# Five re-orderings on single engines in a one-core trunk layer: a gate pair's products, the rounding of k, two copies, one gated product

## The chip, the cores and the metric

The kernel runs on one core of one Trainium2 chip. The time is the device time of one execution in microseconds (us), and of several executions the median is taken. The core's engines run side by side: TensorE (PE in the profile) multiplies matrices, with its weight load shown apart as PEld; VectorE (DVE) and ScalarE (ACT) do elementwise work; GpSimd (POOL) does some elementwise work and issues some of the transfers; SyncE (SP) issues most of them. Each engine works through its own instruction list in order, and waits at an instruction until what it needs has been signalled.

## The reference, cut to what matters

One layer of a streaming encoder, on 512 tokens of 1024 channels, all in float32:

```
h    = rms_norm(x);   xa, ga, q, k, v, f, gA, gB = split(h @ w_in)
y_a  = gelu(ga) * rg_lru(causal_conv4(xa))              # recurrent branch, width 1280
y_b  = softmax(q k^T / 8 + cum[i] - cum[j], causal) @ v  # 16 heads of 64
m    = sigmoid(gA + bA) * (y_a @ w_proj_a) + sigmoid(gB + bB) * (y_b @ w_proj_b)
x    = x + rms_norm(m @ w_out)
u    = causal_conv3(rms_norm(x) @ w_up)                  # 1024 -> 6144
gate, val = split(u)
x    = x + rms_norm((gelu(gate) * val) @ w_down)         # 3072 -> 1024
```

The change touches four products: `h @ w_in` for the gates gA and gB, q and k of the attention, `@ w_up`, and the last block of `gelu(gate) * val`, which is an input of `@ w_down`.

## The kernel before, in words

**High and low halves.** Every float32 operand of a matmul is split in two tiles: a rounded one (`h`, cast on ACT) and the remainder (`l`, subtracted on DVE: value minus rounded value). A product takes three matmuls: high by high, high by low, low by high. Each block of weights therefore passes through an SP transfer into a `raw_` tile, an ACT cast into `wh_` and a DVE subtraction into `wl_` (class `Split`). `fetch(i)` issues these three for all blocks up to number i of one long list; `unit(name)` takes a block for use and fetches two blocks beyond it, so for q of pair p + 1 that of pair p + 2. In some stages the remainder comes in another way (`plain_low`): ACT writes the negated raw tile into `ml`, and a transfer on POOL's queue adds the raw data onto it.

**Products in pairs.** Gates and up-projection take two output tiles (128 channels by 512 tokens each) together as a `Pair`, with seven products of half the inner size in place of eight, from sums of weight blocks (`sums`, tiles `t`, `th`, `tl`) and sums of inputs (`sh`, `sl`). Each product is 12 matmuls of 256 columns (L405, L406, L408). They go into two PSUM banks, `p.a` and `p.c`. Between them intermediate results are copied out by ACT (`keep`, L412, tiles `x0`, `x1`, `x2`; `gx` in the gates) and added back by DVE (`add`, L424). `p5` starts bank `c`; `p12` does products 1 and 2 in bank `a`, of which `keep(2)` then copies one half, and `add` adds it to the other before `product(6)` goes on there. One `period` (L429) interleaves the products of pair p with the last product and the epilogue of the pair before (`b`), and with the splitting of the weights of the next two (`n1`, `n2`). In the first period there is no pair before it (`b` is empty). In the gates (L911 to L945) and in the up-projection (from L1315) the order of all instructions on each engine is the order in which the program issues them (a manual schedule).

**Attention.** It runs over eight pairs of heads, p = 0 to 7. In each turn `scores` (L980) multiplies q and k of pair p, q and k of pair p + 1 are projected (`project`, 24 matmuls of 512 columns each, L218 to L220), and then `halves` (L963) turns the finished PSUM banks into `h_q`, `l_q`, `h_k`, `l_k`: a rounding copy on ACT (L966) and a subtraction on DVE (L967). `scores` of the next pair needs all four. It multiplies high by high, high by low and low by high into three banks per head (`s0a`, `s0b`, `s0c` for head 0). Here the order on each engine isn't written by hand: the tile layer's planner sets it, from the program's order and what it reckons to be ready. `prep_alloc` prepares the attention's biases, `tg_load` loads gate tiles that `gate_epilogue` had stored as `gmb`.

**Up-projection and down-projection.** The epilogue of an up pair is a convolution of three taps (ACT L1267, DVE L1273), a GELU on ACT (L1277), and `glu` (L1279): the product of both halves on POOL (L1281, tile `yf`), stored to DRAM (`yd`) by a transfer on SP's queue, for the last block, j = 23, on POOL's. The down-projection is 42 steps of 12 matmuls (L1387 to L1389). Step i needs its weights (`wh_dn`, `wl_dn`) and its inputs `ah` and `al`, split by ACT (L1361) and DVE from tiles loaded back out of `yd` (`yr` for the first six steps, and `q` or its sums behind them).

Of the kernel before, what the change touches and what calls it, by code (L numbers as in the profile page):

```python
# [12 lines left out]
ALU = mybir.AluOpType  # L13
# [12 lines left out]
JF = DF // P  # L26
# [37 lines left out]
def kernel(  # L64
# [16 lines left out]
    act, dve, pool, pe = nc.scalar, nc.vector, nc.gpsimd, nc.tensor  # L81
# [3 lines left out]
    def offset(stack, n, side="left"):  # L85

        places[0] += 1
        pool = stack.enter_context(tc.tile_pool(name=f"offset{places[0]}", bufs=1, side=side))
        pool.tile([P, n // 4], F32, name=f"offset{places[0]}")
# [9 lines left out]
    def bank(name):  # L99
        return pspools[-1].tile([P, 512], F32, tag="ps", name=name)  # L100
# [98 lines left out]
    where = {name: i for i, (name, _, _) in enumerate(order)}  # L199
    ready, emitted, special = {}, [0], {}  # L200

    def fetch(i):
        while emitted[0] <= min(i, len(order) - 1):
            n, src, shape = order[emitted[0]]
            w = Split(src, shape, n, special.get(n))
            w.hi()
            w.lo(dve)
            ready[n] = w.parts()
            emitted[0] += 1

    def unit(name, ahead=2):

        i = where[name]
        fetch(i + ahead)
        return ready.pop(name)

    def mm3(dst, ah, al, bh, bl, first, last):
        pe.matmul(dst, ah, bh, start=first, stop=False)  # L218
        pe.matmul(dst, ah, bl, start=False, stop=False)  # L219
        pe.matmul(dst, al, bh, start=False, stop=last)  # L220

    def project(dst, unit, ah, al, lo=0, hi=S):
        wh, wl = unit
        for k in range(KD):
            mm3(dst[:, lo:hi], wh[:, k], wl[:, k], ah[:, k, lo:hi], al[:, k, lo:hi], k == 0, k == KD - 1)
# [56 lines left out]
    hh = hpool.tile([P, KD, S], F32R, name="hh")  # L282
    hl = hpool.tile([P, KD, S], F32R, name="hl")
# [32 lines left out]
    def sub(out, a, b):  # L316
        dve.tensor_tensor(out=out, in0=a, in1=b, op=ALU.subtract)  # L317

    A, B = slice(0, 512), slice(512, 1024)
    X, Y = slice(0, SH), slice(SH, S)  # L320
# [109 lines left out]
    def period(p, b, n1, n2, epilogue, load):  # L430

        if b:
            p.p5()
            b.add(b.c[:, Y], b.a[:, Y], 1)
            b.add(b.c[:, X], b.c[:, X], 0)
        n1.plain(1)
        if b:
            epilogue(b, "c", 0)
            p.keep(1, p.c[:, X])
            n1.sums(0)  # L440
        p.product(6, p.a[:, Y])
        if b:
            n1.sums_hi(0)
        p.keep(0, p.a[:, Y])
        if b:
            epilogue(b, "c", 1)
            n1.sums(1)
            b.product(4, b.a[:, Y])
            epilogue(b, "a", 0)
            n1.sums_lo(0)  # L450
        n2.plain_low(0)
        if b:
            n1.sums_hi(1)
        p.product(3, p.c[:, X])
        if b:
            epilogue(b, "a", 1)
        n2.plain_high(0)
        n1.p12()
        if b:
            n1.sums_lo(1)  # L460
        if isinstance(n1, Pair):
            n1.keep(2, n1.a[:, Y])
        if b:
            epilogue(b, "a", 2)
        if isinstance(n1, Pair):
            n1.add(n1.a[:, X], n1.a[:, X], 2)
        load()
        epilogue(b, "a", 3)
        p.product(7, p.a[:, Y])

    with ExitStack() as rg:
        rt, ixt, tt = {}, {}, {}
        last_act = [None]
        with ExitStack() as r0:
# [208 lines left out]
            for t in range(NF, TR + NF):  # L683
# [3 lines left out]
                if t < TR:  # L687
                    ps = bank(f"xa{t}")
# [154 lines left out]
        for step, (e, half) in enumerate(PA_ORDER):  # L843
# [3 lines left out]
            for i in range(5):  # L847
                k = 5 * half + i
# [48 lines left out]
    with ExitStack() as g2:  # L897
        spool = g2.enter_context(tc.tile_pool(name="gsums", bufs=1, side="right", reuse_waits="tile"))
        gates.sh = [spool.tile([P, KH, SH], F32R, name=f"gsh{i}") for i in range(4)]
        gates.sl = [spool.tile([P, KH, SH], F32R, name=f"gsl{i}") for i in range(4)]  # L900
        gp[1] = Pair(gates, 1, GP[1])
        man = g2.enter_context(ExitStack())
        man.enter_context(tc.manual_schedule())
        for i, f in enumerate((fq[3], fq[0], fq[2], fq[1])):
            act.copy(gates.sh[i], f)
            sub(gates.sl[i], f, gates.sh[i].bitcast(F32))
        hfstk.close()
        st0pool = splitstk.enter_context(tc.tile_pool(name="gsplit0", bufs=2, side="right", reuse_waits="tile"))
        offset(splitstk, 448, "right")
        st1pool = splitstk.enter_context(tc.tile_pool(name="gsplit1", bufs=2, side="right", reuse_waits="tile"))  # L910
        gates.stpools = [st0pool, st1pool]  # L911
        none = Nothing()
        p, n = gp[0], gp[1]
        p.plain_high(0)
        p.plain_high(1)
        p.p5()
        p.p12()
        n.sums(0)
        n.sums(1)
        n.plain_low(0)  # L920
        p.keep(2, p.a[:, Y])
        p.add(p.a[:, X], p.a[:, X], 2)
        p.keep(1, p.c[:, X])
        n.sums_hi(0)
        n.sums_lo(0)
        n.sums_hi(1)
        n.sums_lo(1)
        n.plain_high(0)
        gp[2] = Pair(gates, 2, GP[2])

        def more(j):
            if j + 3 < len(GP):
                gp[j + 3] = Pair(gates, j + 3, GP[j + 3])
            elif j + 2 < len(GP):
                pass
            else:
                fetch(where[("q0", "k0")[j + 2 - len(GP)]])

        for j in range(len(GP)):
            period(gp[j], gp.get(j - 1), gp.get(j + 1, none), gp.get(j + 2, none), gate_epilogue, lambda: more(j))  # L940
            gp.pop(j - 1, None)
        splitstk.close()
        sumstk.close()
        bpool = bstk.enter_context(tc.tile_pool(name="bias", bufs=2, reuse_waits="tile"))
        bias = prep_alloc(0)  # L945
        b = gp.pop(len(GP) - 1)
        b.add(b.c[:, Y], b.a[:, Y], 1)
        b.add(b.c[:, X], b.c[:, X], 0)
        gate_epilogue(b, "c", 0)
        pq = bank("q0")  # L950
        project(pq, unit("q0", 0), hh, hl)
        gate_epilogue(b, "c", 1)
        pk = bank("k0")
        project(pk, unit("k0", 0), hh, hl)
        b.product(4, b.a[:, Y])
        gate_epilogue(b, "a", 0)
        gate_epilogue(b, "a", 1)

    with ExitStack() as at:
# [3 lines left out]
        def halves(ps, name):  # L963
            hi = apool.tile([P, S], F32R, tag=f"{name[0]}h", name=f"h_{name}", bufs=1)
            lo = apool.tile([P, S], F32R, tag=f"{name[0]}l", name=f"l_{name}", bufs=1)
            act.copy(hi, ps)  # L966
            dve.tensor_tensor(out=lo, in0=ps, in1=hi.bitcast(F32), op=ALU.subtract)  # L967
            return hi, lo

# [82 lines left out]
        def pb_part(e, ks):  # L1052
            if e not in pb:
                pb[e] = bank(f"pb{e}")
                pbw[e] = unit(f"pb{e}", 1)
            wh, wl = pbw[e]
            for k in ks:
                mm3(pb[e], wh[:, k], wl[:, k], yb[k][:, 0], yb[k][:, 1], k == 0, k == KD - 1)

        q, k = halves(pq, "q0"), halves(pk, "k0")  # L1060
        prev = None
        for p in range(KD):
            now = scores(p, q, k, bias)
            if p < KD - 1:
                bias = prep_alloc(p + 1)
                pq = bank(f"q{p + 1}")
                project(pq, unit(f"q{p + 1}"), hh, hl)
            else:
                pb_part(0, range(KD - 2))
            if prev is not None:  # L1070
                pts = pt(p - 1, prev)
            if p < KD - 1:
                pk = bank(f"k{p + 1}")
                project(pk, unit(f"k{p + 1}"), hh, hl)
                q, k = halves(pq, f"q{p + 1}"), halves(pk, f"k{p + 1}")
            else:
                pb_part(1, range(KD - 2))
            if prev is not None:
                av(p - 1, pts)
            normalise(now)  # L1080
            prev = now
# [196 lines left out]

    def glu(j, g, v):  # L1279
        y = ypool.tile([P, S], F32, tag="yf", name=f"yf{j}", bufs=2)  # L1280
        pool.tensor_tensor(out=y, in0=g, in1=v, op=ALU.mult)  # L1281
        (nc.gpsimd if j == JF - 1 else nc.sync).dma_start(yd[j // 2][:, j % 2], y)

    def up_epilogue(b, which, step):
# [25 lines left out]
    def first_glu(j):  # L1310
        gelu(fe[j][0])
        glu(j, *fe[j])
# [3 lines left out]
    p, n = pairs[NU], pairs[NU + 1]  # L1316
# [76 lines left out]
    def load(j):  # L1393
        if j + 3 < JF:
            pairs[j + 3] = up_pair(j + 3)
        elif j == JF - 2:
            for i in range(2):
                load_w(i)
                load_first(i)

    with man2:
# [3 lines left out]
        b, p = pairs.pop(JF - 2), pairs.pop(JF - 1)  # L1405
# [51 lines left out]
        q = {}  # L1457
# [207 lines left out]
```

## Time and profile before

| | before |
|---|---|
| time of three runs, us | 924.07, 925.25, 927.36 (median 925.25) |
| profiled execution: its time, its span, us | 925.07, 923.2 |
| PE busy | 907.4 us, 98% |
| PE's weight loads | 802.3 us, 87% |
| DVE busy | 722.3 us, 78% |
| ACT busy | 598.3 us, 65% |
| POOL busy | 222.0 us, 24% |
| transfers | 187.07 MB, 203 GB/s over the span |

The shares are of the span, from the first to the last instruction of that execution. Rows of the timeline give the start within the span, the duration, the engine, the line of the kernel, the operation, the tiles as output<-input, shapes, and in brackets the idle time of the engine just before it with what ended it. Tile names are shortened to their letters, so `ma` stands for every tile of that name, and `x4` at the end of a row means four instructions in a row. Matmuls overlap: one is shown longer than the distance to the next.

### The profile page before, as it was taken

What the parts mean: (1) busy time and instruction counts of PE and PEld (TensorE: products, weight loads), DVE (VectorE), ACT (ScalarE), POOL (GpSimd) and SP (SyncE); (2) the same over time, 40 slices, a digit from 0 to 9 for tenths busy, and PEclk for the clock granted to TensorE, in tenths of its full rate; (3) what the DMA queues carried; (4) which work ended last, traced back from release to release, by engine and by line L of the source; (5) the groups of instructions that cost most, each with busy time, mean ns of one, the idle gap of its engine ahead of it and who ended that gap; (6) DMA issues with size and microseconds to landing.
All of it is one profiled execution on the core that took longest, in us unless ns stands there. A gap on an engine that the chain in (4) does not pass through costs nothing.

```text
span 923.2 us, 15775 instructions
## 1 busy us (share of the span) xinstructions
PE 907.4 (98%) x5834; PEld 802.3 (87%) x5834; DVE 722.3 (78%) x1184; ACT 598.3 (65%) x1033; POOL 222.0 (24%) x282
## 2 busy tenths in 40 slices
PE   8999999999999999999999999999999999999996
PEld 7988888878889987888888889999999999978885
DVE  5866369638767657888877588999999999879897
ACT  7555495433467646677654376698888888667664
POOL 4134345434111113112103200042323323100001
PEclk9999999999999999999999999999999999999999
DMA  7677679989877776335324654189888988799764
GB/s 275 220 228 203 171 183 270 255 226 198 197 185 181 187 259 222 121 126 165 136 101 146 207 183 160 36 215 232 220 235 202 241 206 210 226 362 324 249 202 141
DMA packets 71615, 187.07 MB, mean 203 GB/s; under 512 B 7217, under 2 KB 27489, under 8 KB 71154
## 3 DMA queue, kind: packets, MB, share of 16 engines
q1 hardware_dynamic: 47360, 127.33, 41.2%
q0 software_dynamic: 23888, 58.20, 29.0%
q8 instruction: 46, 0.75, 0.3%
q10 hardware_dynamic: 290, 0.53, 0.2%
q14 instruction: 31, 0.25, 0.1%
HBM read 150.69 MB, written 35.73 MB: 202 GB/s over the span
## 4 chain that ended last, share of the span: by engine, by line
PE 92%; DMA 2%; DVE 2%; issue 1%; ACT 1%; SPq 1%; POOL 0%; DVEq 0%; ACTq 0%; POOLq 0%
PE up L408 7%; PE up L406 7%; PE up L405 7%; PE dn L1389 4%; PE dn L1388 4%; PE dn L1387 4%; PE pa L218 2%; PE ga L219 2%; PE ga L218 2%; PE pa L220 2%; PE pa L219 2%; PE ga L220 2%; PE q L218 2%; PE k L218 2%; PE pb L218 2%; PE wo L1128 2%
## 5 line engine op out<-in xcount | busy, mean ns | idle before, releaser
L1273 DVE SCALAR_TENSOR_TENSOR u<-up,cpt,u 128x511 f32<-128x511 f32 x96 | 71.2, 745 | 2.6 <-ACT u L1267 0.9
L353 POOL DMA_DIRECT2D ml<-raw_up x41 | 35.2, 860 | 155.1 <-ACT ml L352 79.3
L1389 PE MATMUL dn<-wh_dn,al 128*128 128x512 f32 x168 | 65.6, 390 | 0.8 <-DVE al L317 0.8
L1387 PE MATMUL dn<-wh_dn,ah 128*128 128x512 f32 x168 | 65.4, 389 | 0.0
L1388 PE MATMUL dn<-wl_dn,ah 128*128 128x512 f32 x168 | 65.4, 389 | 0.0
L405 PE MATMUL up<-sh,th 128*128 128x256 f32 x252 | 60.5, 277 | 0.5 <-ACT x L412 0.5
L406 PE MATMUL up<-sl,th 128*128 128x256 f32 x252 | 60.4, 276 | 0.0
L175 DVE TENSOR_TENSOR wl_dn<-raw_dn,wh_dn 128x1024 fp32r<-128x1024 f32 x42 | 51.4, 1225 | 8.4 <-ACT wh_dn L172 8.3
L172 ACT CAST wh_dn<-raw_dn 128x1024 fp32r<-128x1024 f32 x42 | 44.1, 1050 | 17.4 <-issue 6.9
L317 DVE TENSOR_TENSOR tl<-t,th 128x1024 fp32r<-128x1024 f32 x42 | 51.1, 1217 | 1.3 <-ACT th L387 1.3
L1267 ACT ACTIVATE u<-up,cpt 128x512 f32<-128x512 f32 x48 | 36.9, 778 | 20.1 <-PE up L408 10.8
L1281 POOL TENSOR_TENSOR yf<-u,u 128x512 f32<-128x512 f32 x24 | 32.1, 1338 | 71.1 <-issue 47.1
L405 PEld LDWEIGHTS up<-sh,th 128*128 128x128 f32 x252 | 47.3, 188 | 0.7 <-ACT x L412 0.7
L406 PEld LDWEIGHTS up<-sl,th 128*128 128x128 f32 x252 | 47.3, 188 | 0.0
L387 ACT CAST th<-t 128x1024 fp32r<-128x1024 f32 x42 | 43.9, 1045 | 4.5 <-DVE t L317 1.6
L405 PE MATMUL up<-h2h,mh 128*128 128x256 f32 x168 | 40.2, 276 | 0.0
L406 PE MATMUL up<-h2l,mh 128*128 128x256 f32 x168 | 40.2, 276 | 0.0
L408 PE MATMUL up<-sh,tl 128*128 128x256 f32 x252 | 38.9, 276 | 0.0
L994 ACT ACTIVATE P<-P,mx 128x384 f32<-128x384 f32 (+2 forms) x64 | 35.2, 552 | 5.5 <-DVE mx L989 4.6
L1389 PEld LDWEIGHTS dn<-wh_dn,al 128*128 128x128 f32 x168 | 31.5, 188 | 8.1 <-DVE al L317 1.7
L1388 PEld LDWEIGHTS dn<-wl_dn,ah 128*128 128x128 f32 x168 | 31.5, 188 | 6.5
L1387 PEld LDWEIGHTS dn<-wh_dn,ah 128*128 128x128 f32 x168 | 31.5, 188 | 6.5
(716 smaller groups left out, 3253.8 us busy)
## 6 DMA issues: line engine op xcount, KB each, us to landing
raw_up<-in_w_up_dram SPq DMA_DIRECT2D x48, 512.0 KB, 5.4
td<-in_w_down_dram POOLq DMA_DIRECT2D x36, 512.0 KB, 6.0
raw_dn<-td SPq DMA_DIRECT2D x24, 512.0 KB, 5.0
B<-cnd POOLq DMA_DIRECT2D x16, 640.0 KB, 5.4
ml<-raw_up POOLq DMA_DIRECT2D x20, 512.0 KB, 5.6
raw_dn<-in_w_down_dram SPq DMA_DIRECT2D x18, 512.0 KB, 4.0
raw_wo<-in_w_out_dram SPq DMA_DIRECT2D x16, 512.0 KB, 4.0
td<-td POOLq DMA_DIRECT2D x12, 512.0 KB, 11.3
```

The lines of the kernel that those rows point to most:

```text
L172: act.copy(self.wh, self.raw)
L175: engine.tensor_tensor(out=self.wl, in0=self.raw, in1=self.wh.bitcast(F32), op=ALU.subtract)
L218: pe.matmul(dst, ah, bh, start=first, stop=False)
L317: dve.tensor_tensor(out=out, in0=a, in1=b, op=ALU.subtract)
L387: act.copy(self.th[i], self.t[i])
L405: pe.matmul(dst, wh[:, k], ah[:, k], start=first and k == 0, stop=False, skip_group_check=True)
L406: pe.matmul(dst, wh[:, k], al[:, k], start=False, stop=False, skip_group_check=True)
L408: pe.matmul(dst, wl[:, k], ah[:, k], start=False, stop=k == KH - 1, skip_group_check=True)
L1273: dve.scalar_tensor_tensor(out=c[:, s:], in0=ps[:, : S - s], scalar=col(C_CFW + 3 * e + j), in1=c[:, s:], op0=ALU.mult, op1=ALU.add)
L1387: pe.matmul(dst[t], ah[:, k, tok], wh[:, k], start=first, stop=False, skip_group_check=True)
L1388: pe.matmul(dst[t], ah[:, k, tok], wl[:, k], start=False, stop=False, skip_group_check=True)
L1389: pe.matmul(dst[t], al[:, k, tok], wh[:, k], start=False, stop=last, skip_group_check=True)
```

## The change

It moves instructions at five places. No arithmetic is added or removed.

1. First gate pair (L916, L917): `p12` is issued ahead of `p5`.
2. `period` (L429): in the first period of a stage (`b` empty) `product(6)` and `keep(0)` are issued ahead of `n1.plain(1)`. PE's order stays. On ACT the copy `keep(0)` goes ahead of the negation and the cast of `plain(1)`, in the gates and in the up-projection.
3. Rounding of k in the attention: each rounding copy of `halves` is recorded, and `behind` takes the next weight block only after the latest of them. So on ACT `h_k` of pair p goes ahead of the cast of a weight of pair p + 2 (of q for the first pair, of k for the next; at p = 6 of a block of `w_proj_b`), and on DVE `l_k` goes ahead of that weight's remainder. An explicit `fetch` ahead of the loop keeps the blocks up to k of pair 1 where they were. The planner's order shifts with it in two places more: on PE two products of the scores of the first pair and of the second stand in another order among themselves, and two q matmuls that stood between the scores of the second pair stand behind them; on SP one load of `tg` and one store of `gmb` go ahead of the loads of the fifth pair's raw q and k.
4. The last `glu` (j = 23): the product is issued on VectorE in place of POOL. There it stands behind the subtraction `al` of the fifth down step. Its store stays on POOL's queue.

```diff
@@ period @@
+        if not b:
+            p.product(6, p.a[:, Y])
+            p.keep(0, p.a[:, Y])
         n1.plain(1)
         if b:
             epilogue(b, "c", 0)
             p.keep(1, p.c[:, X])
             n1.sums(0)
-        p.product(6, p.a[:, Y])
-        if b:
+            p.product(6, p.a[:, Y])
             n1.sums_hi(0)
-        p.keep(0, p.a[:, Y])
+            p.keep(0, p.a[:, Y])
@@ first gate pair @@
         p.plain_high(1)
+        p.p12()
         p.p5()
-        p.p12()
@@ attention @@
         def halves(ps, name):
...
-            act.copy(hi, ps)
+            rounded.append(act.copy(hi, ps))
...
+        rounded = []
+
+        def behind(name):
+            with tc.issue_after(rounded[-1].ins):
+                return unit(name)
+
         q, k = halves(pq, "q0"), halves(pk, "k0")
+        fetch(where["k1"])
...
-                project(pq, unit(f"q{p + 1}"), hh, hl)
+                project(pq, (unit if p else behind)(f"q{p + 1}"), hh, hl)
...
-                project(pk, unit(f"k{p + 1}"), hh, hl)
+                project(pk, behind(f"k{p + 1}"), hh, hl)
@@ last gated product @@
-        pool.tensor_tensor(out=y, in0=g, in1=v, op=ALU.mult)
+        (dve if j == JF - 1 else pool).tensor_tensor(out=y, in0=g, in1=v, op=ALU.mult)
```

## Prediction

> **What bounds the kernel now.** I read the page's totals first, then the view of what each engine waits for, then the timeline around each of the five places.
>
> ```profile
> span 923.2 us, 15775 instructions
> PE 907.4 (98%) x5834; PEld 802.3 (87%) x5834; DVE 722.3 (78%) x1184; ACT 598.3 (65%) x1033; POOL 222.0 (24%) x282
> ```
>
> TensorE (PE) is busy 98% of the span, the next engine 78%. The change removes no matmul, so it can win only the stretches in which PE stands still, and lose only where it adds one. The view of waits lists them for PE (us in total, times, longest):
>
> ```profile
> PE s2c L980 <- ACT h_k L966: 1.4, 1, 1.4
> PE ma L405 <- DVE ma L424: 0.9, 1, 0.9
> PE dn L1389 <- DVE al L317: 0.8, 1, 0.8
> PE s0c L980 <- DVE l_k L967: 0.6, 1, 0.6
> PE up L405 <- ACT x L412: 0.5, 1, 0.5
> PE up L408 <- DMA ml<-raw_up: 0.3, 1, 0.3
> ```
>
> Five of these stand at the places of the change; the sixth stands 8.6 us behind one of them. A wait is a little more than its idle time: matmuls issue every 0.227 us (512 columns) or 0.113 to 0.118 us (256) while each is shown longer, so I count from issue to issue; and the first matmul after a stop holds the next one up by another 0.11 us.
>
> **Part 1: order of the first gate pair.** Step `p12` (24 matmuls of tile `ma0`) goes ahead of `p5` (12 of `ma1`). Columns: start, duration, engine, line, operation, output<-input; the idle time before it in brackets.
>
> ```profile
> 264.48 0.63 PE L408 MATMUL ma<-hh,gml 128*128 128x256 f32 x4
> 265.14 0.65 ACT L412 COPY gx<-ma 128x256 f32<-128x256 f32 x2 [3.54 <-PE ma L408]
> 265.55 0.43 DVE L424 TENSOR_TENSOR ma<-ma,gx 128x256 f32<-128x256 f32 x1 [3.21 <-ACT gx L412]
> 265.67 2.02 ACT L387 CAST gth<-gt 128x1024 fp32r<-128x1024 f32 x2
> 266.03 0.39 PE L405 MATMUL ma<-gsh,gth 128*128 128x256 f32 x1 [0.93 <-DVE ma L424]
> 267.57 1.06 ACT L361 CAST gmh<-raw_ma 128x1024 fp32r<-128x1024 f32 x1
> 268.87 0.28 PE L405 MATMUL ma<-hh,gmh 128*128 128x256 f32 x1
> ```
>
> Both steps are issued by 264.48 + 4 x 0.118 = 264.95 in either order. Today `ma0` is done last, its copy (`gx`, 265.14) and its sum (DVE, to 265.98) follow, and `product(6)` starts at 266.03: 1.08 us lost. With `p12` first, `ma0` is done 12 x 0.118 = 1.4 us sooner, at about 263.70; copy and sum end near 264.6, and `product(6)` starts at 264.95. But the second copy (`gx1`, of `ma1`) now waits for `p5`, so the ACT queue behind it moves up only by the one copy that it no longer has there: from about 265.05 `gx1` runs 0.36, to 265.41, where today the first `gth` cast starts at 265.67. That is 0.26, for the two `gth` casts and `gmh` behind them, which ends at 268.37 for 268.63. `product(6)` and `product(3)` take 2 x 12 x 0.1135 = 2.72, so PE wants `gmh` (at 268.87 today) from 267.67 and gets it at 268.37 + 0.05 = 268.42. It is late next. Gain: 268.87 - 268.42 less 0.11 for the stop = **0.34**. Ends: 0 (a copy later) and 1.08 (the cast not late). The DMAs of this part stay where they are.
>
> **Part 2: the copy `keep(0)` ahead of `plain(1)` in the first period of both stages.** In the gates it moves ahead of two ACT instructions and nobody waits for it: `product(7)`, which overwrites what it reads, comes 36 matmuls later, some 4 us; 0. In the up-projection it is the wait of 607.11:
>
> ```profile
> 605.12 0.63 ACT L1277 ACTIVATE u<-u 128x512 f32<-128x512 f32 x1
> 605.84 1.70 POOL L1281 TENSOR_TENSOR yf<-u,u 128x512 f32<-128x512 f32 x1 [6.48 <-ACT u L1277]
> 605.98 0.62 PE L408 MATMUL up<-h2h,ml 128*128 128x256 f32 x4
> 606.69 0.36 ACT L412 COPY x<-up 128x256 f32<-128x256 f32 x1
> 607.11 0.39 PE L405 MATMUL up<-sh,th 128*128 128x256 f32 x1 [0.51 <-ACT x L412]
> 608.31 7.33 DMA ml<-raw_up
> 615.68 0.74 PE L408 MATMUL up<-h2h,ml 128*128 128x256 f32 x4 [0.34 <-DMA ml<-raw_up]
> ```
>
> The copy now follows the GELU directly: 605.75 to 606.11. PE can go on at 605.98 + 4 x 0.113 = 606.43 for 607.11, 0.67 sooner. Eight microseconds on it needs the `ml` tile that this transfer brings at 615.64. The chain of waits leads back from it over the POOL queue: the product `yf` (from 605.84, behind the GELU), one transfer, then this one at 608.31. The change moves none of these: the ACT half of `ml1` slips by that one copy, and POOL is busy with `yf` until 607.54 anyhow. So PE arrives 0.67 earlier and waits 0.67 longer: **0**. Ends: 0 and the whole 0.67, if that transfer comes in 0.67 shorter:
>
> ```profile
> ml<-raw_up POOLq DMA_DIRECT2D x20, 512.0 KB, 5.6
> ```
>
> where 5.6 us is the median of 20 such transfers from issue to landing, so 7.33 is a long one.
>
> **Part 3: rounding of k.** The ACT copy `h_k` goes ahead of the next weight's cast, and DVE's `l_k` ahead of its remainder. First pair, then second, then third:
>
> ```profile
> 339.54 0.39 PE L220 MATMUL k<-hh,wl_k 128*128 128x512 f32 x1
> 340.74 0.58 ACT L966 CAST h_k<-k 128x512 fp32r<-128x512 f32 x1
> 341.37 0.50 PE L980 MATMUL s0c<-h_k,h_q 64*128 64x512 f32 x1
> 342.00 0.68 DVE L967 TENSOR_TENSOR l_k<-k,h_k 128x512 fp32r<-128x512 f32 x1
> 344.27 0.50 PE L218 MATMUL q<-hh,wh_q 128*128 128x512 f32 x1
> 355.07 0.39 PE L220 MATMUL k<-hh,wl_k 128*128 128x512 f32 x1
> 355.26 1.04 ACT L172 CAST wh_k<-raw_k 128x1024 fp32r<-128x1024 f32 x1 [3.58 <-PE k L219]
> 356.22 0.58 ACT L966 CAST h_k<-k 128x512 fp32r<-128x512 f32 x1
> 359.77 0.50 PE L220 MATMUL q<-hh,wl_q 128*128 128x512 f32 x1
> 374.50 0.50 PE L980 MATMUL s4c<-h_k,h_q 64*128 64x512 f32 x1
> 376.70 0.50 PE L218 MATMUL q<-hh,wh_q 128*128 128x512 f32 x1
> ```
>
> The third pair shows undisturbed scores: 376.70 - 374.50 = 2.20 us. The first takes 344.27 - 341.37 = 2.90, because `l_k` ends at 342.68. After the change `h_k` starts when k is done (339.93) and `l_k` ends near 341.3, ahead of its use at 341.37 + 0.37. Gain 2.90 - 2.20 = **0.70**, and 0.03 because the start no longer waits. In the second pair `h_k` starts at 355.49 for 356.22, so scores start 0.73 sooner, at 356.12; `l_k` then ends at 356.8, 0.18 after PE wants it; scores and the two q matmuls of that stretch take 2.20 + 0.18 + 0.57 to 359.07, for 359.77: **0.70**. In the other five pairs PE has other matmuls between k and the scores; only some 0.03 each: **0.1**. What is pushed back: the weight casts by one copy (0.5 us), their remainders by 0.7 to 1.3, and so the loads of raw q and k on the SP queue, where also one load of `tg` and one store of `gmb` come ahead of two of them, by about as much. A weight is cast two pairs (some 28 us) ahead of its use, which covers it; without that cover it would be 0.5 to 1.3 a pair. Sum 1.53; ends 0.9 (the second pair alone and little else) and 1.65.
>
> **Part 4: the last gated product on VectorE.** One instruction leaves POOL and joins DVE behind `al` of the fifth step of the down-projection; its store stays on the POOL queue.
>
> ```profile
> 810.20 1.43 POOL L1281 TENSOR_TENSOR yf<-u,u 128x512 f32<-128x512 f32 x1 [8.98 <-issue]
> 810.39 1.78 DVE L317 TENSOR_TENSOR al<-yr,ah 128x512 fp32r<-128x512 f32 x1
> 812.23 0.50 PE L1389 MATMUL dn<-wh_dn,al 128*128 128x512 f32 x1 [0.82 <-DVE al L317]
> 815.77 0.62 ACT L1361 CAST ah<-q 128x512 fp32r<-128x512 f32 x1 [3.30 <-DMA q<-yd]
> 816.42 0.69 DVE L317 TENSOR_TENSOR al<-q,ah 128x512 fp32r<-128x512 f32 x1 [1.38 <-ACT ah L1361]
> 817.35 0.39 PE L1387 MATMUL dn<-wh_dn,ah 128*128 128x512 f32 x1
> ```
>
> While POOL works from 810.20 to 811.63 a subtraction that takes 0.69 at 816.42 takes 1.78. Alone it ends at 811.08, before PE wants it (0.98 before 812.23, at 811.25). That is 0.98, and 0.11 for the stop: 1.09. DVE then does `yf`, which no row shows; I take 0.69, the row of `al` at 816.42, also two 512-column inputs from SBUF on DVE (ends: that and POOL's 1.43). It ends at 811.77, or 812.51, and DVE, which today is held by the stretched `al` until 812.17, is free 0.4 sooner or 0.3 later; with 1.43 the next remainder could cost PE up to 0.3 of the gain. The store behind it goes out when DVE is done, 0.14 after today's 811.63 or 0.9 after, and no other store or load stands behind it on its queue. Next late is the seventh step: it begins at 817.35, in the new time 816.26, and needs `ah` of the first loaded q, which ends at 816.39 and is set by a load. It starts at 816.44, and its third matmul waits for `al` (817.11): with two stops of 0.11, 0.56 of the 1.09 is lost. Gain **0.53**; ends 0 and 1.09.
>
> **Sum.** 0.34 + 0 + 1.53 + 0 + 0.53 = 2.4 us. The profiled execution took 925.07 (span 923.2 and 1.9 around it), 0.18 under the median of three, 925.25. 925.07 - 2.4 = **922.6**, rounded down. Least: 0 + 0 + 0.9 + 0 + 0 = 0.9; most: 1.08 + 0.67 + 1.65 + 1.09 = 4.5.
>
> **The rivals.**
> - *The late-next waits do not come.* Three of my discounts (`gmh` 0.74, the `ml` transfer 0.67, q 0.56) rest on transfer or queue times of one execution. For: the long `ml` transfer. Against: the order in the three DMA queues around them is what it was. With one or two gone the gain is 3.0 to 4.0: 921 to 922.
> - *Absorbed.* Where transfers set the pace, PE's earlier arrival is waited away again, as with `ml` in part 2. For: the gains of parts 1 and 3 have two more stages to get through. Against: of PE's waits listed above one ends on a transfer, and only with 0.3. Half of parts 1 and 3 lost leaves 1.5: 923.6; that the gains vanish altogether, by this or because the stops come back in another place: 925.
> - *Slower: the weight of the next pair comes late.* Each pair's two weights are cast when PE's last matmul on the old ones frees the buffer (355.26, after `PE k L219`). Part 3 puts copy and remainder ahead of that, so cast, remainder, the release of the raw tile and its next load all start 0.5 to 1.3 later in each of six pairs. Nothing is lost while the 28 us of cover hold; if the load turned out to be the slowest link, the delay would pass to PE, 3.0 to 7.8 in all, less the 0.34 and 0.53 of the other parts: 927.2 to 932, taken at 928.5. Against: no wait of q's or k's matmuls on a weight stands in the list. It decides once more than 27 of the 28 us are used up.
> - *The store of the last product collides with the load of q* (a smaller loss). The seventh step has 0.96 of slack today (816.39 to 817.35) and none after the change, so each microsecond by which that load lands later is paid. A store of half a load's size can take at most its own share: if the load comes 1 later, part 4 gives nothing and 0.5 is lost: 923.6. The Trainium skill (DMA: Bandwidth & Descriptors, section "Issuing engines are not separate DMA queues") says that transfers started by any engine run on the same 16 DMA engines and interleave; by that rule the POOL queue is no shelter for the store, and the sum of part 4 would come to -0.5 in place of 0.53. The trace has the two side by side today as well, so I keep it as a part of the case "absorbed".
>
> **How the numbers follow.** About 0.3% (2.8 us, so 922.47 from the median) is what a measurement of this kernel can tell from no change; my sum lies just short of it. The sum as worked: 0.42, its own range 921.9 to 923.3, half of it on either side of the line. Late waits gone: 0.28, faster. Absorbed, the collision with it, or no change at all: 0.17, within. Slower by the weights: 0.13, nearly all of it beyond the line. Faster 0.21 + 0.28 = 0.49; within 0.21 + 0.17 = 0.38; slower 0.13. The range runs from all stops gone (925.07 - 4.5 = 920.6, a little below) to nothing left: 920.4 to 925.3.
>
> **What would show it.** Right: no wait of PE at the first gate sum, at the two `s0c`/`s2c`, at the `x` copy and at the fifth `al`, whose time is 0.7; in their place a wait of about 0.7 on the cast `gmh`, one of about 1.2 on the `ml` transfer, and a short one on the first q. Wrong: if a removed wait stays, if the `ml` transfer lands earlier, or if PE waits where it does not today, on a weight of q or k above all.

## The result, and the profile after

The changed kernel took 923.76 us in the median of 22 runs (921.26 to 926.41), the kernel before 925.66 in 22 runs (924.07 to 927.88). The ratio is 0.9978, with a 95% interval of 0.9970 to 0.9986: 2.0 us faster, clear of no change and less than the 0.3% that I had set as the bound of "faster". The profiled execution took 923.54, against 925.07.

The page's first lines of the changed kernel, and below them the view of what PE waits for (us in total, times, longest):

```profile
span 921.8 us, 15768 instructions
PE 908.2 (99%) x5834; PEld 803.9 (87%) x5834; DVE 723.0 (78%) x1185; ACT 598.4 (65%) x1033; POOL 218.5 (24%) x281
```

```profile
PE up L408 <- DMA ml<-raw_up: 0.8, 1, 0.8
PE s2c L982 <- ACT h_k L968: 0.7, 1, 0.7
PE dn L1396 <- ACT ah L1370: 0.5, 1, 0.5
...
PE ma L405 <- ACT gmh L361: 0.5, 1, 0.5
...
PE up L405 <- DVE up L424: 0.4, 1, 0.4
```

Four of the five stops of before are gone (gate sum, `l_k`, the copy `x`, the fifth `al`); that on `h_k` has fallen from 1.4 to 0.7. Three have come or grown in their place: the cast `gmh`, the `ml` transfer (0.3 to 0.8) and `ah` of the first loaded q. All three are the ones that the prediction named as late next. A fourth was not foreseen: the sum `up` on VectorE.

To see where the time went, I compare when PE issues the same matmul, counted by its number, in two executions. The executions differ by up to 2.7 us before any changed line. The first halo product of the gates shows it in the kernel before and in two kernels that are the same up to there:

```profile
44.90 0.47 PE L529 MATMUL gate<-halo_h,gh 96*128 96x512 f32 x1 [0.61 <-DMA halo_h<-xl]
```

```profile
46.49 0.47 PE L531 MATMUL gate<-halo_h,gh 96*128 96x512 f32 x1 [0.68 <-DMA halo_h<-xl]
```

```profile
43.82 0.47 PE L529 MATMUL gate<-halo_h,gh 96*128 96x512 f32 x1
```

So the table takes off each execution's difference at 52 us; each row is one execution. It gives how much later (+) or earlier (-) than the kernel before PE was, in us, at six matmuls; column heads are their times before and the stage that has just ended. Labels are those of the experiments below.

| kernel | 339 gates | 449 scores of pair 6 | 583 | 605 first up period begins | 631 first up periods | 862 down-projection under way |
|---|---|---|---|---|---|---|
| changed | -0.44 | -2.77 | -2.50 | -1.71 | -1.16 | -1.19 |
| e1_gate | -0.27 | -0.19 | -0.12 | +0.68 | +0.57 | +0.57 |
| e2_k | -0.01 | -2.37 | -2.36 | -2.36 | -2.37 | -2.37 |
| e3_copy | +0.04 | +0.05 | +0.07 | +0.07 | +0.23 | +0.25 |
| e4_yf | -0.01 | +0.10 | +0.09 | +0.09 | +0.53 | +0.19 |
| v1_gate | -1.16 | -3.49 | -3.26 | -2.47 | -2.23 | -1.37 |
| v2_up | -0.13 | -2.49 | -2.27 | -2.27 | -0.11 | +0.35 |
| v3_q | -0.42 | -2.75 | -2.56 | -2.56 | -2.01 | -3.09 |
| v4_all | -1.14 | -3.51 | -3.24 | -2.44 | -0.58 | -1.65 |
| x1_gate_q | -1.15 | -3.48 | -3.23 | -2.43 | -2.30 | -3.39 |
| x2_no_copy | -1.13 | -3.48 | -3.41 | -2.61 | -2.33 | -3.40 |
| x3_sub | -1.16 | -3.51 | -3.33 | -3.33 | -2.24 | -3.31 |
| x4_pool | -1.16 | -3.52 | -3.28 | -2.49 | -1.41 | -1.42 |

The changed kernel is 2.77 ahead by 449 us, and then loses: 0.27 up to 583, 0.79 from 583 to 605, 0.55 in the first up periods. Part 4 nets nothing. The last three are looked at below. Of the 0.27, 0.19 is lost at one matmul of `pb` near 479 us, in the changed kernel and in all kernels built on it but x2_no_copy; why is open, and no run was made for it.

### The profile page after: what moved, and what is told of

Read it like the earlier page. It is cut to its first block, busy times and chain, and to the rows that moved or that the text cites. A ratio compares the mean times of both kernels' runs of the same rounds, so it can differ in the third digit from the quotient of the medians.

```text
span 921.8 us, 15768 instructions
## 1 busy us (share of the span) xinstructions
PE 908.2 (99%) x5834; PEld 803.9 (87%) x5834; DVE 723.0 (78%) x1185; ACT 598.4 (65%) x1033; POOL 218.5 (24%) x281
## 4 chain that ended last, share of the span: by engine, by line
PE 93%; DMA 2%; DVE 2%; issue 1%; ACT 1%; POOL 0%; SPq 0%; DVEq 0%; ACTq 0%; POOLq 0%
PE up L408 7%; PE up L406 7%; PE up L405 7%; PE dn L1398 4%; PE dn L1396 4%; PE dn L1397 4%; PE pa L218 2%; PE ga L219 2%; PE ga L218 2%; PE pa L220 2%; PE pa L219 2%; PE ga L220 2%; PE q L218 2%; PE k L218 2%; PE wo L1137 2%; PE pb L219 2%
```

## The experiments

### Each part alone

My theory was the prediction's: a stop that is removed stays won, unless the next operand is late. The rival says that the up-projection's transfers take back what is won ahead of it. The four kernels are the kernel before with one part each.

**e1_gate**

```diff
+        p.p12()
         p.p5()
-        p.p12()
```

> Only p12 ahead of p5 in the first gate pair. Theory A (each stop removed stays won unless the next operand is late): in the trace the 1.09 us stop at the gate sum is gone, a stop of 0.5 to 0.65 on the cast gmh stands 2 us behind it, PE is 0.4 earlier at the end of the gates (about 340 us) and 0.4 at the end of the span: ratio 0.9996. Theory B (what is won ahead of the up-projection is given back there to the ml transfer): 0.4 earlier at 340, nothing at 620.

Ratio 0.9997 (0.9984 to 1.0010). PE's stop at the gate sum is gone, and 2 us on stands

```profile
268.82 0.39 PE L405 MATMUL ma<-hh,gmh 128*128 128x256 f32 x1 [0.48 <-ACT gmh L361]
```

as expected. From 263 to 339 us it gains 0.42 (in the changed kernel 0.41). From 583 to 605 it loses 0.80; that loss isn't of this part, and is taken up under the hardware.

**e2_k**

```diff
...
+            rounded.append(act.copy(hi, ps))
...
+                project(pk, behind(f"k{p + 1}"), hh, hl)
...
```

> Only the rounding of k. Theory A: the stop on l_k in the first pair is gone, that on h_k in the second falls from 1.55 to 0.9, PE is 1.5 to 1.8 earlier from 360 us on and stays so to the end, since the transfers of the up-projection start earlier with it: 923.9, ratio 0.9983. Theory B: 1.5 to 1.8 earlier at 570, but under 1 earlier at 620. Theory C (the loss of 0.7 between 577 and 602 in the changed kernel is PE issuing 256-column matmuls every 117.8 in place of 113.3 ns, by chance of the short stop at 577): either value can come, with the same stop in front.

Ratio 0.9969 (0.9957 to 0.9980), 2.9 us: as good as the whole change. The trace has 2.37 at 449 us and still 2.37 at 862, so nothing is given back, and the rival (theory B) falls. It is more than the 1.53 worked out. One of the later pairs shows what was left out; first before, then e2_k:

```profile
391.51 0.68 DVE L967 TENSOR_TENSOR l_k<-k,h_k 128x512 fp32r<-128x512 f32 x1
...
391.88 0.50 PE L980 MATMUL s6c<-h_k,h_q 64*128 64x512 f32 x1
...
392.25 0.50 PE L980 MATMUL s6c<-l_k,h_q 64*128 64x512 f32 x1
...
392.59 0.39 PE L980 MATMUL s6c<-h_k,l_q 64*128 64x512 f32 x1
```

```profile
390.00 0.49 PE L980 MATMUL s6c<-h_k,h_q 64*128 64x512 f32 x1
...
390.33 0.39 PE L980 MATMUL s6c<-l_k,h_q 64*128 64x512 f32 x1
...
390.56 0.39 PE L980 MATMUL s6c<-h_k,l_q 64*128 64x512 f32 x1
```

From the first to the third product it is 0.71 before and 0.56 in e2_k. A restart behind a late `l_k` cost 0.15 in this pair: before, `l_k` ends at 392.19, just ahead of its use at 392.25; in e2_k it ends 1.3 us ahead. The restart is too short to stand in the view of waits, but it comes in each of the five later pairs, and the trace has 0.66 between 365 and 449 us. The eighth pair, whose rounding isn't moved, keeps its 0.71 (0.70 in e2_k).

**e3_copy**

```diff
+        if not b:
+            p.product(6, p.a[:, Y])
+            p.keep(0, p.a[:, Y])
         n1.plain(1)
...
```

> Only the copy keep(0) ahead of plain(1) in the first periods. Theory A and B alike: the stop of 0.67 at 607.1 goes, and the ml transfer takes it back some 8 us on (stop of 0.5 grows to 1.1 or more): 0 at 620 and at the end, ratio 1.0. If the transfer does not take it back: 0.6 earlier at 620, ratio 0.9993.

Ratio 1.0007 (0.9997 to 1.0016). The stop of 0.67 is gone, and two others take it back; from 605 to 631 us 0.16 is lost in all:

```profile
611.36 0.38 PE L405 MATMUL up<-sh,th 128*128 128x256 f32 x1 [0.42 <-DVE up L424]
```

```profile
617.72 0.39 PE L408 MATMUL up<-h2h,ml 128*128 128x256 f32 x1 [0.86 <-DMA ml<-raw_up]
```

The second is the one predicted. The first comes earlier: PE now reaches the next `product(6)` sooner than the sum on VectorE that has to come before it. What holds that sum is shown by v2_up, below.

**e4_yf**

```diff
-        pool.tensor_tensor(out=y, in0=g, in1=v, op=ALU.mult)
+        (dve if j == JF - 1 else pool).tensor_tensor(out=y, in0=g, in1=v, op=ALU.mult)
```

> Only the last gated product on VectorE. As predicted: the stop of 0.98 at the fifth al goes, two stops of 0.56 in all come back at the seventh step on ah and al of the first loaded q, 0.5 earlier at the end, ratio 0.9994. As the trace of the changed kernel reads (0.97 won, 0.94 lost): 0 to 0.1, ratio 1.0.

Ratio 0.9999 (0.9991 to 1.0008). In the trace PE is 0.34 earlier at 862 than at 631 us: the stop at `al` is gone, and 0.75 of its 1.09 comes back in the seventh step. In the changed kernel 1.06 comes back there.

### What stands in the way next

The three stops that came in place of the removed ones are each attacked by one more move on top of the changed kernel.

**v1_gate**

```diff
-        p.keep(1, p.c[:, X])
         n.sums_hi(0)
         n.sums_lo(0)
+        p.keep(1, p.c[:, X])
```

> The changed kernel with one more move: in the first gate pair the cast gth of sums_hi(0) and its remainder go ahead of the copy keep(1). Theory A (the order on ACT makes gmh late): the stop of 0.64 on gmh is gone or under 0.2, PE 0.5 to 0.75 earlier at 340 us than the changed kernel: against before some 2.5 in all, ratio 0.9973. Rival (gth cannot start earlier, its buffer or its sum is what is late): the stop stays at 0.64, ratio as that of the changed kernel, 0.9978.

Ratio 0.9970 (0.9957 to 0.9983). ACT of the changed kernel, then of v1_gate:

```profile
264.91 0.37 ACT L412 COPY gx<-ma 128x256 f32<-128x256 f32 x1 [1.04 <-PE ma L408]
265.18 2.00 ACT L387 CAST gth<-gt 128x1024 fp32r<-128x1024 f32 x2
267.07 1.05 ACT L361 CAST gmh<-raw_ma 128x1024 fp32r<-128x1024 f32 x1
```

```profile
263.78 1.05 ACT L387 CAST gth<-gt 128x1024 fp32r<-128x1024 f32 x1
264.93 0.37 ACT L412 COPY gx<-ma 128x256 f32<-128x256 f32 x1
265.19 1.05 ACT L387 CAST gth<-gt 128x1024 fp32r<-128x1024 f32 x1
266.14 1.05 ACT L361 CAST gmh<-raw_ma 128x1024 fp32r<-128x1024 f32 x1
```

ACT stood idle for 1.04 us behind a copy that waited for PE, with a cast behind it that was ready. With the cast first, `gmh` ends 0.93 earlier and the stop is gone: -1.16 at 339 us, against -0.44. Part 1 is then worth all of its 1.08. But the gain isn't kept: at 862 us this kernel is 1.37 ahead of the one before, the changed kernel 1.19. In the first up periods it loses less than that one, and then 0.86 from 631 to 862 us, where the first load of q takes 6.04 us (5.21) and the stop on `ah` behind it grows from 0.5 to 1.3.

**v2_up**

```diff
             p.keep(0, p.a[:, Y])
+            n2.plain_low(0)
         n1.plain(1)
...
-        n2.plain_high(0)
         n1.p12()
...
             n1.keep(2, n1.a[:, Y])
+        n2.plain_high(0)
```

(in the first up period only)

> The changed kernel with the first up period's ACT work in another order: the negation for ml of the pair after next goes ahead of plain(1), its cast mh behind the copy x2. Theory A (the ml transfer is late because ACT issues its first half 1.2 us behind the GELU and the copies, and the add waits for x2 behind mh): the stops of 0.51 (add) and 1.01 (ml transfer) go to under 0.3 in all, 1.2 more than the changed kernel: ratio 0.9965. Rival (the transfer keeps its landing whatever the issue, since the DMA engines are shared): the stop on ml stays at 0.8 or more, ratio 0.9975 to 0.998.

Ratio 0.9988 (0.9977 to 1.0000): worse than the changed kernel in the trace by 1.6 between 605 and 631 us. The wait on the transfer of the other `ml` tile takes the place of the one removed, and the transfer after next is late as well:

```profile
614.35 0.39 PE L408 MATMUL up<-sh,ml 128*128 128x256 f32 x1 [1.96 <-DMA ml<-raw_up]
```

```profile
615.44 10.95 DMA ml<-raw_up
626.38 0.04 issue
626.43 0.62 PE up L408 x3
```

Neither expectation holds as it stands. The order on ACT sets which of the two transfers goes first: the one moved ahead lands at 613.05 us and is used at 615.85 without a wait, and the one behind it lands at 614.30. Against the same matmuls (this execution is 0.69 later at 605) that is 1.9 earlier and 1.8 later than in the changed kernel. When the two can start isn't set by ACT: in the changed kernel's chain of waits the late `ml` transfer is issued by POOL behind the product `yf`, and takes 7.94 us itself:

```profile
603.86 1.03 POOL yf L1290
604.89 0.58 issue
605.47 0.85 POOL ml L353
606.32 7.94 DMA ml<-raw_up
```

The stop at the sum stays too, 0.52 for 0.51, although the copy `x2` comes sooner. The changed kernel, then v2_up:

```profile
604.27 2.97 DVE L1282 SCALAR_TENSOR_TENSOR u<-up,cpt,u 128x511 f32<-128x511 f32 x4
606.87 0.37 ACT L412 COPY x<-up 128x256 f32<-128x256 f32 x1
607.27 1.23 DVE L424 TENSOR_TENSOR up<-up,x 128x256 f32<-128x256 f32 x3
```

```profile
605.08 2.97 DVE L1288 SCALAR_TENSOR_TENSOR u<-up,cpt,u 128x511 f32<-128x511 f32 x4
606.68 0.38 ACT L412 COPY x<-up 128x256 f32<-128x256 f32 x1
607.97 1.22 DVE L424 TENSOR_TENSOR up<-up,x 128x256 f32<-128x256 f32 x3
```

The stopped matmul starts at 607.75 and at 608.45. The copy starts 0.88 ahead of it in one and 1.77 in the other, the sum 0.48 in both. So the copy doesn't hold the sum; the four instructions of the convolution that stand ahead of it on VectorE do: they end within 0.1 us of its start.

**v3_q**

```diff
         for i in range(3, len(STEPS)):
+            if i == 3:
+                for m in range(3):
+                    load_22(m)
             load_w(i + 5)
```

(left out above: the three loads are taken from their old place, behind that weight load)

> The changed kernel with the first three loads of q ahead of the weight load that the SP queue waits with. Theory A (q lands late because its issue stands behind that wait): the stops of 0.65 and 0.27 at the seventh down step are gone, part 4 keeps its 0.97: ratio 0.9969. Rival (the loads wait for their space or share the engines as before): a stop of 0.5 or more stays, on q or on the weight that was pushed back, ratio 0.9978.

Ratio 0.9957 (0.9940 to 0.9974). In the changed kernel the chain starts at the load, and the load starts where SP gets past a weight load that waits; in v3_q ACT has the tile 4.3 us earlier, of which 1.7 is that execution's lead at 805 us:

```profile
809.54 5.21 DMA q<-yd
...
814.85 0.63 ACT ah L1370
815.48 0.04 issue
815.52 0.50 PE dn L1396
```

```profile
810.55 0.62 ACT L1370 CAST ah<-q 128x512 fp32r<-128x512 f32 x1 [1.15 <-DMA q<-yd]
```

From 631 to 862 us PE gains 1.08, where the changed kernel gains 0.03. No stop of over 0.2 us stands in the down-projection any more.

**v4_all**: the three moves together.

> All three further moves. If they add: 2.4 below the changed kernel, 921.3, ratio 0.9952; if the rivals hold, 0.9975.

Ratio 0.9969 (0.9959 to 0.9979). They don't add: the move in the up-projection costs 1.9 between 605 and 631 us, where the kernel without it (x1_gate_q) loses 0.13.

### The better version, and two parts undone in it

**x1_gate_q**: the changed kernel with the moves of v1_gate and v3_q.

> The changed kernel with the gate cast moved ahead and the q loads moved ahead, without the further move in the up-projection. The two gains at their places (0.62 at 268 us, 0.9 at the seventh down step) add to the changed kernel's: 2.1 + 1.5 = 3.6 below before, ratio 0.996; no stop of over 0.3 at 268 or behind 805. If the up-projection gives the gate's gain back: 0.9967.

Ratio 0.9960 (0.9948 to 0.9972), 922.19. Both gains stand at their places: -1.15 at 339 us, and 1.09 between 631 and 862.

**x2_no_copy**: that kernel with the `period` of before.

```diff
-        if not b:
-            p.product(6, p.a[:, Y])
-            p.keep(0, p.a[:, Y])
```

> The kernel just above without the copy keep(0) ahead of plain(1) (the period of before). If the copy is worth nothing, because the add behind x2 and the ml transfer take its 0.65 back: from the gates' end to 640 us this kernel takes as long as the one above within 0.2, ratio equal within 0.0005, with one stop of 0.67 at the copy and a smaller one at ml in place of the two at the add and ml. If the copy is worth its 0.67: this kernel is 0.6 later at 640 us, ratio 0.0007 higher.

Ratio 0.9952 (0.9937 to 0.9967), 921.38, the lowest of all; it lies below the changed kernel's interval altogether, but not below those of x1_gate_q and v3_q. Without the copy's move PE loses 0.28 between 605 and 631 us, with it 0.13. Its waits stand at the old places, the one at `ml` at 0.8 for 0.3:

```profile
PE up L408 <- DMA ml<-raw_up: 0.8, 1, 0.8
...
PE up L405 <- ACT x L412: 0.4, 1, 0.4
```

So part 2 is worth 0.15 here and cost 0.16 in e3_copy: nothing, within what the traces differ by. How much they do in that stretch x4_pool shows, below: its code there is that of x1_gate_q, and it loses 1.07 for 0.13.

**x3_sub**: x1_gate_q with one `ml` tile made by VectorE.

```diff
-        n2.plain_low(0)
-        n2.plain_high(0)
...
             n1.add(n1.a[:, X], n1.a[:, X], 2)
+        n2.plain_high(0)     # makes the remainder by a subtraction
```

(in the first up period only)

> The kernel with gate and q moves, and the one late ml tile of the first up period made by a subtraction on VectorE, without its transfer. If that transfer alone holds PE there: the stop of 1.0 at ml goes and nothing takes its place, 1 us earlier at 640 us, ratio 0.001 lower than without. If the stage is as tight on VectorE (busy 19.7 of 20 us): a stop of 0.5 or more moves to an add or to a product behind VectorE, same ratio or higher.

Ratio 0.9957 (0.9945 to 0.9969), the same as without. The stop at that tile is gone. A new one comes on VectorE, and the next pair's transfer takes the rest:

```profile
607.30 0.38 PE L405 MATMUL up<-h2h,th 128*128 128x256 f32 x1 [0.34 <-DVE up L424]
```

```profile
622.23 0.38 PE L408 MATMUL up<-h2h,ml 128*128 128x256 f32 x1 [0.84 <-DMA ml<-raw_up]
```

From 605 to 631 us it loses 1.09. The first up periods are held by more than one transfer; three kernels have moved the stop and none has removed it.

**x4_pool**: x1_gate_q with the last gated product on POOL.

> The kernel with gate and q moves, and the last gated product back on POOL. If part 4 is worth its stop as soon as the q loads are early: the stop of 0.98 at the fifth al stands again, and this kernel is 0.9 to 1.1 later behind it, ratio 0.001 higher. If the early loads alone bring the gain: same ratio, and the stop at al is hidden by something later.

Ratio 0.9960 (0.9948 to 0.9972): in the runs the same as x1_gate_q, since 0.1% is less than these intervals can tell. The trace can: from 631 to 862 us this kernel gains nothing, x1_gate_q 1.09. The stop is back:

```profile
808.64 1.32 POOL L1290 TENSOR_TENSOR yf<-u,u 128x512 f32<-128x512 f32 x1 [9.09 <-issue]
```

```profile
808.72 1.79 DVE L317 TENSOR_TENSOR al<-yr,ah 128x512 fp32r<-128x512 f32 x1
```

```profile
810.56 0.50 PE L1398 MATMUL dn<-wh_dn,al 128*128 128x512 f32 x1 [0.79 <-DVE al L317]
```

Early loads alone bring 0. Part 4 alone brings 0.34 (e4_yf) and 0.03 (the changed kernel), and in v2_up and v1_gate, which have it without the early loads, 0.46 and 0.86 are lost. Both together bring 1.09. The Trainium skill (SBUF — State Buffer, section "SBUF: two separate sides") says that GpSimd and VectorE lock a pair of ports that they share, VectorE for an instruction with two inputs from SBUF while GpSimd reads SBUF too, and that the one that starts later is blocked until the other is done. By that `al`, with its own 0.69 behind `yf`, would end at an estimated 808.64 + 1.32 + 0.69 = 810.65; the trace has 808.72 + 1.79 = 810.51. It agrees within 0.14.

## Why the prediction was right, and where it wasn't

Forecast were 922.6 us and a gain of 2.4 in one execution against another. The medians differ by 1.9 and the ratio gives 2.0; the two profiled executions differ by 1.4 in span and 1.5 in time, and by 1.19 once the difference of their first 52 us is taken off. The time and the sign were right, and so was the mechanism of each part. That the sum came this near is in part luck: part 3 gave 0.8 more than worked out and part 4 0.5 less, and 1.6 was lost at places for which the sum has no term. The largest chance, 0.49, stood on a gain of over 0.3%; measured is 0.22%, in the case that had 0.38.

- **Part 1, forecast 0.34: measured 0.41.** The stop, its successor (the cast `gmh`, 2 us on) and the reason (the copy `gx1`, which waits for `p5`, ahead of the casts on ACT) were as worked out. v1_gate shows the reason by taking it away.
- **Part 2, forecast 0: measured +0.16 alone, -0.15 in x1_gate_q.** The `ml` transfer took the time back, as said; the sum on VectorE, behind the convolution, took a part of it first, which the step did not see.
- **Part 3, forecast 1.53: measured 2.33 to 2.37.** The step of the working that failed is "The third pair shows undisturbed scores: 376.70 - 374.50 = 2.20 us". They were not undisturbed. In the changed kernel the same stretch is

```profile
372.18 0.49 PE L982 MATMUL s4c<-h_k,h_q 64*128 64x512 f32 x1
```

```profile
374.24 0.50 PE L218 MATMUL q<-hh,wh_q 128*128 128x512 f32 x1
```

  2.06: each pair of before held a restart of some 0.14 behind `l_k`. It is missing twice in the sum. In "the other five pairs [...] only some 0.03 each: 0.1" it makes 0.66, and in the first pair, measured against that 2.20, 0.96 for 0.73. The second gave 0.74, for 0.70. (Five times 0.03 is 0.15, not 0.1; that slip is small beside the rest.) The list of signs names the stop at `s2c` as gone, but the working takes only 0.73 off it, and that is what came: 1.4 to 0.7.
- **Part 4, forecast 0.53: measured 0.34 alone, 0.03 in the whole change.** The stop was worth its 1.09 (x1_gate_q against x4_pool) and the late-next operand was the one named. The term for what is lost, 0.56, was 0.75 in one execution and 1.06 in the other, where the load took 4.88 and 5.21 us; with 5.71 in v2_up and 6.04 in v1_gate more was lost than the stop had cost. The term rests on one execution's load, and that time isn't steady. The row for `yf` on VectorE, taken as 0.69, is 0.69.

```profile
809.62 0.69 DVE L1290 TENSOR_TENSOR yf<-u,u 128x512 f32<-128x512 f32 x1
```

- **Not forecast: 0.79 lost from 583 to 605 us**, to a slower issue of matmuls (next section), **and 0.55 in the first up periods**: the stop of 0.67 went, stops of 0.51 at the sum and 0.20 at one `ml` tile came, and that at the other `ml` tile grew from 0.51 to 1.01. The waits on transfers there vary from execution to execution: e4_yf, which changes nothing in that stage, lost 0.44 in it, and e2_k nothing.
- **The rivals.** "The late-next waits do not come" falls: all three came. "Absorbed" was a part of the truth, in the up-projection and at the q load, but not for part 3, the largest: e2_k keeps its 2.37 to the end. "The weight of the next pair comes late" did not happen: no wait of PE on a weight of q or k stands in the views of the changed kernel or of e2_k. The collision of the store with the load isn't shown: with the store at the same distance behind the load (1.06 us) the load took 4.88 in e4_yf and 6.04 in v1_gate. In the four kernels with the product on POOL and the loads at their old place the store stands 1.0 behind and the load takes 4.6 to 5.0, so that a share of the move in the longer loads can't be ruled out. The store is as large as that load, 256 KB each in the view of transfers, not half of it as the prediction has it.

## What to carry to other kernels

A stop that is removed moves the wait to the next late operand; name that one, and move what holds it in the same step (here part 4 brought between a gain of 0.34 and a loss of 0.86 without the q loads, and 1.09 with them). Look for an instruction that waits at the head of an engine's list while ready work stands behind it: that was the cause at the gates (ACT behind a copy) and in the down-projection (SP behind a weight load). Where an operand is late in a loop, also count the restarts that are too short for a view of waits, and time changes of 0.1% by the trace's same instruction, from a point at which the executions are level, since runs can't tell them.

## What the hardware showed that I had not expected

Matmuls of 256 columns are issued at one of two rates, and stay at it for many microseconds without a stop. The same stretch before and after, from the view of windows (window, its length, PE busy and its matmuls, then the other engines, the granted clock, the share of DMA and GB/s):

```profile
582.00:596.00 14.00, 14.00 (x126) 14.00 (x125) 13.00 (x19) 7.91 (x12) 0.91 (x1) 1.00 0.02 4
```

```profile
582.00:596.00 14.00, 14.00 (x121) 14.00 (x120) 12.54 (x18) 10.28 (x15) 0.91 (x1) 1.00 0.12 34
```

PE is busy throughout at full clock in both, and does 126 matmuls in one and 121 in the other. Between starts it is 113.3 ns in the mean before and 117.8 after. e1_gate, in which no instruction of that stretch differs from before, has it as well:

```profile
582.00:596.00 14.00, 14.00 (x121) 14.00 (x120) 12.62 (x19) 7.47 (x12) 0.91 (x1) 1.00 0.01 2
```

Of the 14 profiles 7 are at the slower rate there (the changed kernel, e1_gate, v1_gate, v4_all, x1_gate_q, x2_no_copy, x4_pool), at a loss of 0.79 to 0.80 us between 583 and 605 in each. The rate is set at a short stop of PE between 576 and 582 us, which all of them have: just ahead of it all go at 113 to 114 ns, behind it some at the one rate and some at the other. The four kernels without part 1 are all at the faster rate and seven of the ten with it at the slower, so that part 1 may have a share in it; what decides is open, and no run was made for it. If it is chance, the two profiled executions stand 0.79 us closer together than the two orders of work would put them.

The kernel before has the slower rate too, a little later: between 605 and 631 us 117 of its 212 matmuls follow the one ahead of them by 117 to 119 ns, in e2_k 8. The faster rate saves e2_k 0.45 there, and its stops are 0.44 longer, so that both take 26.0 us: what PE wins here by issuing faster it waits away at the transfers.
